# A later slot for root scalings, for the closings of the short convolutions and for the base of the inverse, in a hybrid encoder trunk

## The chip, the core and the metric

The kernel runs on one core of one Trainium2 chip. TensorE (PE) does the matmuls, VectorE (DVE), ScalarE (ACT) and GpSimd (POOL) do the rest, SyncE (SP) starts the DMAs. The metric is device time in microseconds (us), the median of several runs. Each engine works through its own queue in program order. An instruction waits in its queue until what it needs is there, and everything behind it on that engine waits with it.

## The reference

One layer for two groups of frames (256 new positions and 64 positions of a running stream, 320 columns together), with a sandwich of RMS norms around two sub-layers. Cut to what matters here:

```python
def gdn_mixer(qkv, z, ...):                       # 8 heads of 128
    qkv = silu(causal_dwconv(qkv, buf, w_sc))     # width 4
    q = l2norm(heads(q)) * HEAD_DIM ** -0.5
    k = l2norm(heads(k))
    o, s = gated_delta_chunked(q, k, v, g, beta, s0)
    o = o * rsqrt(mean(o * o) + EPS) * onorm_g
    return o * silu(z)

def gated_delta_chunked(q, k, v, g, beta, s0):
    m = strict_lower(kb @ k.T * decay)
    tmat = solve(I + m, I)                        # unit lower triangular
    u, w = tmat @ (v * beta), tmat @ (kb * exp(G))
    for each chunk:
        v_new = u - w @ s
        o = (q * exp(G)) @ s + qk @ v_new
        s = s * g_last + k_dec.T @ v_new

def conformer_conv(...):                          # 8 groups of 128 channels
    u = causal_dwconv(h_val * sigmoid(h_gate), width 31)
    return silu(group_layernorm(u))

def trunk_layer(x, ...):
    p = rmsnorm(x) @ w_in
    x = x + rmsnorm(concat(conformer_conv(p), gdn_mixer(p)) @ w_out)
    gu = causal_dwconv(rmsnorm(x) @ w_up, width 3)
    return x + rmsnorm((silu(gate) * up) @ w_down)
```

## The kernel before

Activations lie with channels on the partitions and the 320 columns along the free axis. Each float32 product is made of three: `load_split` loads a weight tile `w` by DMA, ACT rounds it to `whi` (L214) and DVE takes the rest `wlo` (L215). Per 128x128 piece PE then runs whi times the rounded activation (L230), whi times the activation's rest (L231) and wlo times the rounded activation (L234). Each of these is one **dense matmul** of 128x320. `block_matmul` runs 48 of them for each 128 output columns of w_in, and the rest of the layer (w_out, w_up, w_down) works alike.

While w_in runs, in the order of `PLAN`, small steps of the two mixers are threaded between the dense matmuls. They are written as Python generators, called jobs:

- `conv_tail` (one per channel group): transposes into the PSUM tile `pt_c` (L575), statistics on DVE (L577 and after), an inverse square root on POOL (`grs` L583, `gnm` L584), then three scalings on ACT (`un`, L588), and transposes back.
- `gdn_tail` (one per head h0 to h7): transposes of k, q and v (L674 to L678), squares on ACT (L680, L682), `tq6` (L684, L685), the inverse square root and its products on POOL (`sc`, L687 to L693), then the scalings `kd`, `kds` and `vh` on ACT (L697 to L702), then the products `pk`, `pks` (L706, L710) on PE and `np`, `at` on DVE.
- `pair` (one per two heads, pairs 0 to 3): `base_inverse` inverts 16x16 blocks on DVE (L745 to L759, after a trip of `np` through DRAM into `dn`), then after a delay `levels` merges blocks to 32, 64 and 128 on PE and ACT (`pz`, `zh` L784, `px` L789, `zq` L808, `px` L813, ...), then `post` runs the recurrence: `ks` (L872) on PE, `rhs` (L876) on DVE, `pvns` (L884) on PE, `ks1` (L893), `rh1` (L896) on DVE, and so on. It ends with an inverse square root on POOL (`t1`, L921 to L925), the scalings `ot` (L929) on ACT, and, later, the transposes `pt_o` (L938).

The steps share PSUM: the tiles `pt_c`, `pt_c2`, `tkq` and `pt_o` take turns in two banks (pool `ps_t`), and most others in four (pool `ps_g`).

**What sets the order.** `tick` counts the dense matmuls; the text gives places in the program as that count ("dense 1800"). Every `GAP` = 20 dense matmuls it holds a slot: the jobs that are due are advanced by one step each, in a limited number, and each step is issued behind the dense matmul of the slot. A step ends in `yield wait, g, t`: the job is due again `wait` dense matmuls later, at the next slot after that. A fourth value marks the step that follows. A step marked "scale" is one that needs an inverse square root from POOL: it isn't taken in the first loop over the due jobs but in the second one, and is issued behind the newest ACT instruction of the slot. Since the second loop looks at the mark as it stands after the first loop, a job whose step in the first loop has just yielded "scale" is advanced again there, in the same slot: POOL's root and the ACT scaling that needs it are then issued in one slot.

`qkv_block` (three per head) makes a projection and the short convolution: `qb`, `cq` on ACT (L627) and three multiply-adds on DVE (L629), then two SiLU on ACT (L631 to `kq` or `vT`, L632 to `kqs` or `vts`), all issued at once, with raised priority. `conv_block` does a channel group's gate, and its 32 taps (L557 to L560) are handed to DVE a few per slot.

Of the kernel before, what the change touches and what calls it, by code (L numbers as in the profile page):

```python
# [30 lines left out]
GAP = 20  # L31
# [69 lines left out]
def trunk_kernel(ctx, tc, ins, outs):  # L101
# [11 lines left out]
    jobs = []  # L113
# [4 lines left out]
    def next_tap(front=None):  # L118
        left, fn = taps.pop(0)
        with ExitStack() as e:  # L120
            if front is not None:
                e.enter_context(tc.issue_after(front))
            fn()
        left[0] -= 1

    def advance(job, behind=None):
        with tc.issue_after(behind or dense[0]), tc.high_priority(offset=PRI_J):
            try:
                wait, job[2], job[3], *kind = next(job[1])
                job[0] = dense[1] + wait  # L130
                job[4] = kind
            except StopIteration:
                jobs.remove(job)
        return next(i for i in reversed(nc.cur_bb.bb.instructions) if i.engine == dense[0].engine)

    def start(gen, wait, g=0, t=0):
        job = [dense[1] + wait, gen, g, t, []]
        jobs.append(job)
        return job
# [5 lines left out]
    def newest(engine, n0):  # L145
        return next((i for i in reversed(nc.cur_bb.bb.instructions[n0:]) if i.engine == engine), None)

    def tick(mm):
        dense[0] = mm.ins
        dense[1] += 1  # L150
        if dense[1] % GAP == 0:
            g, t0, behind, due = 0, held_t[0], dense[0], []
            t = t0
            n0 = len(nc.cur_bb.bb.instructions)
            for job in sorted(jobs, key=lambda j: j[0]):
                if job[0] <= dense[1] and g + job[2] <= 4 and t + job[3] <= 2:
                    g += job[2]
                    t += job[3]
                    due.append(job)
            for job in due:  # L160
                if not job[4]:
                    behind = advance(job, behind)
            scalar = newest(mybir.EngineType.Activation, n0)
            for job in due:
                if "scale" in job[4]:
                    with ExitStack() as e:
                        if scalar is not None:
                            e.enter_context(tc.issue_after(scalar))
                        advance(job)
            held_t[0] = t - t0  # L170
            front = newest(mybir.EngineType.DVE, n0)
            for _ in range(min(pace[0], len(taps))):
                next_tap(front)
# [15 lines left out]
    def pv(name, a=None, b=None):  # L189
        o, w = PAR[name]  # L190
        if a is None:
            return par[:, o:o + w]
        return par[:, o + a:o + (a + 1 if b is None else b)]
# [103 lines left out]
    def in_block(b, name):  # L297
        if b in ready:
            return ready.pop(b)
        ps = ps_p.tile([P, 512], F32, tag="p", name=name)  # L300
        block_matmul(ps[:, 0:T], ins["w_in"][b], hx, (8, 8))
        return ps
# [10 lines left out]
    with tc.tile_pool(name="xp", bufs=1) as xp:  # L313
# [25 lines left out]
        with tc.high_priority(offset=PRI_E):  # L339
# [25 lines left out]
            for k in range(KB):  # L365
                x = xt[k // 4][:, k % 4, :]
# [32 lines left out]
        def first_norm():  # L399
            rr, _ = rstd([ssum[:, 0, :], ssum[:, 1, :]])  # L400
            yield 36, 1, 0
            S.copy(rb, rstd_rows(rr)[0])

        job = start(first_norm(), 24, 1)
# [10 lines left out]
    gate = {}  # L415
# [185 lines left out]
    NS = 2  # L601
# [16 lines left out]
    def qkv_block(b, dst, dsts, i):  # L618
        psq = in_block(16 + b, "psq")
        qb = qbufs[i % 2]  # L620
        with tc.high_priority(offset=PRI_E):
            S.copy(qb[:, 4, 0:3], pv("s_qkv", b * 3, b * 3 + 3))
            V.tensor_tensor(qb[:, :, 3:67], psq[:, 0:T].rearrange("p (s i) -> p s i", s=5),
                            rb.rearrange("p (s i) -> p s i", s=5), ALU.mult)
            S.copy(qb[:, 1:4, 0:3], qb[:, 0:3, 64:67])
            cq = cb.tile([P, 5, 64], F32, tag="cq", name="cq")
            S.activation(cq, qb[:, :, 0:64], AF.Identity, scale=pv("w_sc", b * 4))  # L627
            for t in range(1, 4):
                V.scalar_tensor_tensor(cq, qb[:, :, t:t + 64], pv("w_sc", b * 4 + t), cq, ALU.mult, ALU.add)  # L629
            S.copy(nqkv[:, b], qb[:, 3:5, 64:67])  # L630
            S.activation(dst, cq[:, 0:4].rearrange("p s i -> p (s i)"), AF.Silu)  # L631
            S.activation(dsts, cq[:, 4], AF.Silu)  # L632

    def gdn_pre(h, st):
        s = h % NS
        while s and h // NS > 1 and "free" not in sts[h // NS - 2]:
            advance(pairs[h // NS - 2])
        if s == 0:
            st["kqs"] = gd.tile([P, 2, P], F32, tag="kqs", bufs=3, name="kqs")
            st["vts"] = gd.tile([P, P], F32, tag="vts", bufs=1, name="vts")  # L640
        kq = gd.tile([P, 2, TP], F32, tag="kq", bufs=5, name="kq")
        vT = gd.tile([P, TP], F32, tag="vT", bufs=1, name="vT")
        cols = slice(s * TS, (s + 1) * TS)
        qkv_block(8 + h, kq[:, 0, :], st["kqs"][:, 0, cols], h)
        qkv_block(h, kq[:, 1, :], st["kqs"][:, 1, cols], h + 1)
        qkv_block(16 + h, vT, st["vts"][:, cols], h)
        return kq, vT


    def gdn_tail(h, st, kq, vT):  # L650
        s = h % NS
        while not gate or (s and "kq" not in st) or (h // NS > 1 and "free" not in sts[h // NS - 2]):
            yield GAP, 1 + 2 * s, 1
        if s == 0:
            st["kd"] = gd.tile([P, S_, P], F32, tag="kd", name="kd")
# [6 lines left out]
        kd, vh, at, kqs = st["kd"], st["vh"], st["at"], st["kqs"]  # L662
# [64 lines left out]
    def base_inverse(bt, st):  # L727
        i = bt % 2
        nb = 8 * NI
        nc.sync.dma_start(nscr[i][:, 0:16384].rearrange("a (p f) -> p a f", f=128), st["np"])  # L730
        dn_t = gd.tile([nb, 272], F32, tag="dn", bufs=1, name="dn")
        wi_t = gd.tile([nb, 272], F32, tag="wi", bufs=1, name="wi")
        tmp_t = gd.tile([nb, 512], F32, tag="tmp", bufs=1, name="tmp")
        dn, wi = (t[:, 0:256].rearrange("p (r c) -> p r c", c=16) for t in (dn_t, wi_t))
        nc.sync.dma_start(dn, blocks(nscr[i], 128))
        G.memset(wi_t, 0.0)
        G.memset(wi_t[:, 0:256:17], 1.0)
        yield 2 * GAP, 0, 0

        d8, w8 = (t.rearrange("p (b x) -> p b x", b=2)[:, :, 0:128].rearrange("p b (r c) -> p b r c", c=16)[:, :, :, 0:8]  # L740
                  for t in (dn_t, wi_t))
        for r in range(6, -1, -1):
            m = 7 - r
            tmp = tmp_t[:, 0:2 * m * m].rearrange("p (b s c) -> p b s c", b=2, s=m)
            V.tensor_tensor(tmp, w8[:, :, r + 1:8, r + 1:8],  # L745
                            d8[:, :, r, r + 1:8].unsqueeze(3).to_broadcast((nb, 2, m, m)), ALU.mult)
            V.tensor_reduce(w8[:, :, r, r + 1:8], tmp.rearrange("p b s c -> p b c s"), AX.X, ALU.add)
            if r in (3, 0):
                yield GAP, 0, 0
        tmp = tmp_t.rearrange("p (r c s) -> p r c s", r=8, c=8)  # L750
        x = dn_t[:, 0:64].rearrange("p (r c) -> p r c", c=8)
        V.tensor_tensor(tmp, dn[:, 0:8, 8:16].unsqueeze(2).to_broadcast((nb, 8, 8, 8)),
                        wi[:, 8:16, 8:16].rearrange("p s c -> p c s").unsqueeze(1).to_broadcast((nb, 8, 8, 8)), ALU.mult)
        V.tensor_reduce(x, tmp, AX.X, ALU.add)
        yield GAP, 0, 0
        V.tensor_tensor(tmp, wi[:, 0:8, 0:8].unsqueeze(2).to_broadcast((nb, 8, 8, 8)),
                        x.rearrange("p s c -> p c s").unsqueeze(1).to_broadcast((nb, 8, 8, 8)), ALU.mult)
        V.tensor_reduce(wi[:, 0:8, 8:16], tmp, AX.X, ALU.add)
        V.tensor_copy(dn, wi.rearrange("p a b -> p b a"))  # L759
        nc.sync.dma_start(blocks(wscr[i], 128)[0:nb], wi)  # L760
        nc.sync.dma_start(blocks(wscr[i], 128)[nb:2 * nb], dn)
        wtp = gd.tile([P, 2, NI, P], F32, tag="wtp", name="wtp")
        nc.sync.dma_start(wtp.rearrange("p a b f -> p (a b) f"), wscr[i][:, 0:16384].rearrange("a (p f) -> p a f", f=128))
        st["w"] = wtp
# [199 lines left out]
    tails, convs, pairs, sts = {}, {}, {}, []  # L964
    for step in plan:
        kind, i = step[0], int(step[1:] or 0)
# [6 lines left out]
        elif kind == "h":  # L973
            if i % NS == 0:
                if i:
                    ready[24 + i] = in_block(24 + i, "psq")
                st = {}
# [147 lines left out]
    job = start(second_norm(), 68, 1)  # L1125
# [189 lines left out]
```

## Time and profile before

| what | value |
|---|---|
| median of 3 runs | 1498.56 us (1497.97 to 1499.13) |
| the profiled execution's own span, first to last instruction | 1497.8 us |
| PE's mean granted clock over it | 0.997 |
| DVE, ACT, POOL busy over the span | 996.1, 727.9, 229.2 us |
| the stretch 38 to 549 us (w_in, the mixers, w_out) | PE busy 501.80 of 511.00 us |
| DMA, mean over the span | 150 GB/s |

The profile counts an engine as busy while an instruction runs; for PE the matmuls are pipelined, so that a dense matmul has a duration of 309 ns in the profile while the next one starts some 147 ns after it. "Idle before" is the time for which an engine stood still ahead of an instruction, with the instruction that ended this. The clock that the profile grants PE is given as a share of full speed, as a mean over a window. Of the time around the profiled span only the difference to the runs' median is known: 1498.56 - 1497.8 = 0.8 us.

### The profile page before, as it was taken

The numbers are of one execution on the slowest core, as the hardware profiler recorded it, in microseconds if no ns is written. First come the engines' busy times: TensorE is split into PE (matmuls) and PEld (weight loads), VectorE is DVE, ScalarE is ACT, GpSimd is POOL, SyncE is SP. The second block draws the span as 40 slices with busy tenths as digits, with TensorE's granted clock in tenths as the row PEclk, the third lists the DMA queues.
The fourth block names the chain that finished last, engine by engine and source line by source line (L and its number), as shares of the span: only waits on it lengthen the run. The fifth ranks groups of instructions, "written<-read, shape, count | busy, mean of one in ns | idle before, by whom it ended". The sixth has DMA issues, their size and how long they took to land.

```text
span 1497.8 us, 27263 instructions
## 1 busy us (share of the span) xinstructions
PE 1481.6 (99%) x10609; PEld 1460.4 (98%) x10610; DVE 996.1 (67%) x1816; ACT 727.9 (49%) x1329; POOL 229.2 (15%) x390
## 2 busy tenths in 40 slices
PE   9999999999999999999999999999999999999998
PEld 8999999989999999999999999999999999999997
DVE  6779886978989678766345666445666545666554
ACT  7764556554544565544434444334444333444453
POOL 0111101120010000332002222002223101222101
PEclk9999999999999999999999999999999999999999
DMA  8435453544434744444554444455444455444453
GB/s 289 142 128 157 141 155 120 146 139 134 130 106 142 221 151 141 148 149 128 149 169 151 151 154 134 140 156 164 154 152 141 136 146 173 153 146 152 130 152 118
DMA packets 98281, 224.22 MB, mean 150 GB/s; under 512 B 18792, under 2 KB 39528, under 8 KB 98152
## 3 DMA queue, kind: packets, MB, share of 16 engines
q1 hardware_dynamic: 98008, 222.45, 47.7%
q8 instruction: 83, 1.36, 0.4%
q14 instruction: 46, 0.38, 0.1%
q10 hardware_dynamic: 144, 0.03, 0.0%
HBM read 215.33 MB, written 7.12 MB: 149 GB/s over the span
## 4 chain that ended last, share of the span: by engine, by line
PE 86%; DVE 6%; ACT 3%; DMA 2%; issue 2%; POOL 1%; SPq 0%; ACTq 0%; DVEq 0%
PE psu L234 13%; PE psu L231 13%; PE psu L230 13%; PE psdn L230 7%; PE psdn L231 6%; PE psdn L234 6%; PE psq L234 2%; PE psq L230 2%; PE psq L231 2%; PE psm L231 2%; PE psm L230 2%; PE psm L234 2%; DVE wlo L215 1%; PE psu L1108 1%; PE ps_first L395 1%
## 5 line engine op out<-in xcount | busy, mean ns | idle before, releaser
L214 ACT CAST whi<-w 128x1024 fp32r<-128x1024 f32 (+2 forms) x440 | 412.6, 940 | 481.7 <-PE psu L231 169.0
L215 DVE TENSOR_TENSOR wlo<-w,whi 128x1024 fp32r<-128x1024 f32 (+2 forms) x440 | 477.0, 1085 | 199.0 <-ACT whi L214 127.8
L230 PE MATMUL psu<-hi,whi 128*128 128x320 f32 x1344 | 397.0, 309 | 0.0
L231 PE MATMUL psu<-lo,whi 128*128 128x320 f32 x1344 | 397.0, 309 | 0.0
L230 PEld LDWEIGHTS psu<-hi,whi 128*128 128x128 f32 x1344 | 252.3, 188 | 0.0
L231 PEld LDWEIGHTS psu<-lo,whi 128*128 128x128 f32 x1344 | 252.3, 188 | 0.0
L234 PE MATMUL psu<-hi,wlo 128*128 128x320 f32 x1344 | 224.4, 309 | 0.0
L234 PEld LDWEIGHTS psu<-hi,wlo 128*128 128x128 f32 x1344 | 204.0, 188 | 0.0
L231 PE MATMUL psdn<-gl,whi 128*128 128x320 f32 x660 | 195.9, 310 | 0.0
L1141 POOL COPY nffn<-fbuf 128x2 f32<-128x2 f32 x88 | 101.5, 1153 | 586.9 <-DVE fbuf L1139 583.7
L1139 DVE TENSOR_TENSOR fbuf<-psu,rb 128x256 f32<-128x256 f32 x88 | 37.3, 424 | 168.9 <-PE psu L234 168.9
L230 PE MATMUL psdn<-gh,whi 128*128 128x320 f32 x480 | 142.8, 309 | 0.0
L231 PEld LDWEIGHTS psdn<-gl,whi 128*128 128x128 f32 x660 | 123.9, 188 | 0.3
L230 PE MATMUL psq<-hh,whi 128*128 128x320 f32 x352 | 106.2, 315 | 0.0
L231 PE MATMUL psq<-hl,whi 128*128 128x320 f32 x352 | 104.1, 309 | 0.0
L230 PEld LDWEIGHTS psdn<-gh,whi 128*128 128x128 f32 x480 | 90.1, 188 | 0.0
L234 PE MATMUL psdn<-gh,wlo 128*128 128x320 f32 x480 | 89.9, 309 | 0.0
L234 PEld LDWEIGHTS psdn<-gh,wlo 128*128 128x128 f32 x480 | 75.3, 188 | 0.0
L230 PEld LDWEIGHTS psq<-hh,whi 128*128 128x128 f32 x352 | 66.1, 188 | 0.3
L231 PEld LDWEIGHTS psq<-hl,whi 128*128 128x128 f32 x352 | 66.1, 188 | 0.2
L560 DVE SCALAR_TENSOR_TENSOR cvt<-ub,par,cvt 128x320 f32<-128x320 f32 x120 | 65.2, 543 | 0.2
L1184 DVE TENSOR_TENSOR y<-y,psdn 128x320 f32<-128x320 f32 x45 | 22.0, 488 | 59.1 <-PE psdn L234 59.1
(356 smaller groups left out, 2483.3 us busy)
## 6 DMA issues: line engine op xcount, KB each, us to landing
w<-in_w_up SPq DMA_DIRECT2D x176, 512.0 KB, 3.6
w<-in_w_in SPq DMA_DIRECT2D x88, 512.0 KB, 3.9
w<-in_w_down SPq DMA_DIRECT2D x64, 384.0 KB, 3.1
w<-in_w_down SPq DMA_DIRECT2D x64, 320.0 KB, 3.0
w<-in_w_out SPq DMA_DIRECT2D x32, 320.0 KB, 3.8
w<-in_w_out SPq DMA_DIRECT2D x16, 384.0 KB, 3.2
w<-in_w_first SPq DMA_DIRECT2D x6, 512.0 KB, 6.9
wtp<-wsp SPq DMA_DIRECT2D x4, 640.0 KB, 6.0
```

What stands on the lines that cost most here:

```text
L214: S.copy(hi[:, 0:width], w[:, 0:width])
L215: V.tensor_tensor(lo[:, 0:width], w[:, 0:width], hi[:, 0:width].bitcast(F32), ALU.subtract)
L230: tick(PE.matmul(ps, wh, xh, start=(first and k0 + j == 0), stop=False))
L231: tick(PE.matmul(ps, wh, xl, start=False, stop=False))
L234: tick(PE.matmul(ps, lo[:, j * P:(j + 1) * P], xh, start=False, stop=(final and k0 + j == nk - 1)))
L395: tick(PE.matmul(ps, w, xh, start=(k == 0 and wt is hi), stop=(k == KB - 1 and wt is lo)))
L560: return lambda: V.scalar_tensor_tensor(acc, x, w, acc, ALU.mult, ALU.add)
L1108: PE.matmul(pss[i][:, 0:T], wt[:, o:o + P], x, start=(k == 0 and n == 0), stop=(k == KB - 1 and n == 2))
L1139: V.tensor_tensor(buf[:, 2:258], psu[:, 0:TP], rb2[:, 0:TP], ALU.mult)
L1141: G.tensor_copy(nffn[:, b, 0, :], buf[:, 256:258])
L1184: V.tensor_tensor(y[:, n, :], y[:, n, :], psd[:, 0:T], ALU.add)
```

## The change

Three edits, in `tick`, in `qkv_block` with `gdn_tail`, and in `base_inverse`.

```diff
@@ tick @@
+            done = []
...
             for job in due:
                 if not job[4]:
                     behind = advance(job, behind)
-            scalar = newest(mybir.EngineType.Activation, n0)
+                    done.append(job)
+            last_of = [i for x in (mybir.EngineType.Activation, mybir.EngineType.DVE)
+                       if (i := newest(x, n0)) is not None]
             for job in due:
-                if "scale" in job[4]:
+                if job[4] and job not in done:
                     with ExitStack() as e:
-                        if scalar is not None:
-                            e.enter_context(tc.issue_after(scalar))
+                        for i in last_of:
+                            e.enter_context(tc.issue_after(i))
                         advance(job)
@@ qkv_block @@
+        def silu():
             S.activation(dst, cq[:, 0:4].rearrange("p s i -> p (s i)"), AF.Silu)
             S.activation(dsts, cq[:, 4], AF.Silu)
+            yield from ()
+
+        job = start(silu(), GAP // 2)
+        job[4] = ["scale"]
+        return job
@@ gdn_pre, gdn_tail @@
-        qkv_block(8 + h, kq[:, 0, :], st["kqs"][:, 0, cols], h)
...
+        return kq, vT, [qkv_block(8 + h, kq[:, 0, :], st["kqs"][:, 0, cols], h),
...
-    def gdn_tail(h, st, kq, vT):
+    def gdn_tail(h, st, kq, vT, silus):
...
-        while not gate or (s and "kq" not in st) or ...
+        while not gate or any(j is silu for j in jobs for silu in silus) or (s and "kq" not in st) or ...
@@ base_inverse (at its first yield, after r = 3 and r = 0, and after L754) @@
-        yield 2 * GAP, 0, 0
+        yield 2 * GAP, 0, 0, "long"
...
-                yield GAP, 0, 0
+                yield GAP, 0, 0, "long"
```

First, a marked step is taken in the second loop only if its job wasn't advanced in the first, so that a root's scaling now waits for a later slot; and it is issued behind the newest ACT and the newest DVE instruction of that slot. Second, the two SiLU that close a short convolution become a job of their own, marked in the same way, due half a gap later; `gdn_tail` doesn't begin before its head's three are done. Third, the steps of `base_inverse` are marked too ("long"), so that they are issued behind the other ACT and DVE steps of their slot. No arithmetic changes. Line numbers grow by 3 to 9: L214 becomes L217, L215 L218, L697 L706, L702 L711, L784 L793, L808 L817, L876 L885.

As the programs are built, the number of instructions on each engine stays as it was but for the loads of ACT's function tables, 9 before and 11 now. The steps on PE stand later in the program: pair 0's and pair 3's chains by 40 dense matmuls, pair 2's by 20 (its first `px` at dense 1800 before, 1820 now), pair 1's by 20 at its begin and 40 at its end. POOL's order is the same.

On ACT, around the first merge of pair 2 (`zh`, then `zq`), this stood before; `vT`, `vts` are SiLU of head 5, the rows from L680 to L702 are head 5's `gdn_tail`:

```order
400 L631 ACTIVATE vT<-cq 128x256
401 L632 ACTIVATE vts<-cq 128x64
402 L784 ACTIVATE zh<-pz,cst 128x80
403 L214 CAST whi<-w 128x1024
...
412 L685 ACTIVATE tq_4133<-ssq_598,eps 128x3
413 L214 CAST whi<-w 128x1024
414 L697 ACTIVATE kd<-tkq,sc 128x128
415 L702 ACTIVATE vh<-tv,sc 128x128
...
420 L808 COPY zq<-pz 32x5x32 x2
421 L214 CAST whi<-w 128x1024
```

And now:

```order
405 L636 ACTIVATE vT<-cq 128x256
406 L637 ACTIVATE vts<-cq 128x64
407 L217 CAST whi<-w 128x1024
408 L793 ACTIVATE zh<-pz,cst 128x80
...
418 L694 ACTIVATE tq_4162<-ssq_598,eps 128x3
419 L217 CAST whi<-w 128x1024
420 L817 COPY zq<-pz 32x5x32 x2
421 L706 ACTIVATE kd<-tkq,sc 128x128
422 L711 ACTIVATE vh<-tv,sc 128x128
...
428 L217 CAST whi<-w 128x1024
```

`zh` has moved one slot down, behind a weight cast, and `zq` has moved ahead of head 5's scalings.

On DVE, around the right-hand side `rhs` of pair 2's recurrence, this stood before; the rows with `tmp`, `dn` and `wi` are the base inverse of pair 3:

```order
514 L752 TENSOR_TENSOR tmp<-dn,wi 40x512
515 L560 SCALAR_TENSOR_TENSOR odd<-ub_587,par,odd 128x320
516 L754 TENSOR_REDUCE dn<-tmp 40x64
517 L876 SCALAR_TENSOR_TENSOR rhs<-ks,neG,vh 64x128
518 L756 TENSOR_TENSOR tmp<-wi,dn 40x512
519 L533 TENSOR_TENSOR sg<-psgate,rb 128x320
520 L876 SCALAR_TENSOR_TENSOR rhs<-ks,neG,vh 64x128
521 L758 TENSOR_REDUCE wi<-tmp 40x8x8
522 L215 TENSOR_TENSOR wlo<-w,whi 128x1024
```

And now:

```order
511 L218 TENSOR_TENSOR wlo<-w,whi 128x1024
...
514 L885 SCALAR_TENSOR_TENSOR rhs<-ks,neG,vh 64x128
515 L563 SCALAR_TENSOR_TENSOR odd<-ub_587,par,odd 128x320
516 L885 SCALAR_TENSOR_TENSOR rhs<-ks,neG,vh 64x128
517 L754 TENSOR_TENSOR tmp<-wi,dn 40x50
...
521 L754 TENSOR_TENSOR tmp<-wi,dn 40x98
522 L218 TENSOR_TENSOR wlo<-w,whi 128x1024
...
525 L761 TENSOR_TENSOR tmp<-dn,wi 40x512
...
527 L763 TENSOR_REDUCE dn<-tmp 40x64
```

Both halves of `rhs` now stand ahead of the last three rows of the recursion and of the four long rows that close the base inverse (L761 to L767, before L752 to L758).

On ACT, around the tails of heads 0 and 1, this stood before; the cast in row 135 makes the first weights of `psz` of block z2, which PE needs at dense 657:

```order
134 L685 ACTIVATE tq_1258<-ssq_597,eps 128x2
135 L214 CAST whi<-w 128x1024
136 L697 ACTIVATE kd<-tkq,sc 128x128
...
140 L680 ACTIVATE vh,ssq_597<-tkq 128x128 x2
...
148 L685 ACTIVATE tq_1316<-ssq_597,eps 128x3
149 L622 COPY qb_594<-par 128x3
```

And now, to the cast that makes the same weights:

```order
133 L694 ACTIVATE tq_1256<-ssq_597,eps 128x2
134 L636 ACTIVATE kq<-cq 128x256
135 L637 ACTIVATE kqs<-cq 128x64
136 L706 ACTIVATE kd<-tkq,sc 128x128
137 L689 ACTIVATE vh,ssq_597<-tkq 128x128 x2
...
142 L694 ACTIVATE tq_1312<-ssq_597,eps 128x3
...
149 L706 ACTIVATE kd<-tkq,sc 128x128
...
158 L637 ACTIVATE kqs<-cq 128x64
159 L217 CAST whi<-w 128x1024 x3
```

The cast that stood ahead of both heads' scalings now stands behind all of them and behind the SiLU of the next short convolution.

More of the change, by code (lines that the diff above doesn't have):

```diff
@@ L643, in gdn_pre @@
         cols = slice(s * TS, (s + 1) * TS)
-        qkv_block(8 + h, kq[:, 0, :], st["kqs"][:, 0, cols], h)
-        qkv_block(h, kq[:, 1, :], st["kqs"][:, 1, cols], h + 1)
-        qkv_block(16 + h, vT, st["vts"][:, cols], h)
-        return kq, vT
-    def gdn_tail(h, st, kq, vT):
+        return kq, vT, [qkv_block(8 + h, kq[:, 0, :], st["kqs"][:, 0, cols], h),
+                        qkv_block(h, kq[:, 1, :], st["kqs"][:, 1, cols], h + 1),
+                        qkv_block(16 + h, vT, st["vts"][:, cols], h)]
+    def gdn_tail(h, st, kq, vT, silus):
         s = h % NS
-        while not gate or (s and "kq" not in st) or (h // NS > 1 and "free" not in sts[h // NS - 2]):
+        while not gate or any(j is silu for j in jobs for silu in silus) or (s and "kq" not in st) or (h // NS > 1 and "free" not in sts[h // NS - 2]):
             yield GAP, 1 + 2 * s, 1
@@ L754, in base_inverse @@
         V.tensor_reduce(x, tmp, AX.X, ALU.add)
-        yield GAP, 0, 0
+        yield GAP, 0, 0, "long"
         V.tensor_tensor(tmp, wi[:, 0:8, 0:8].unsqueeze(2).to_broadcast((nb, 8, 8, 8)),
```

## The prediction

> **What bounds the kernel now.** I read the page's busy times first, then two windows of the span, then PE's waits in the first of them, then PE's granted clock around the two longest waits. PE has almost no idle time:
>
> ```profile
> PE 1481.6 (99%) x10609; PEld 1460.4 (98%) x10610; DVE 996.1 (67%) x1816; ACT 727.9 (49%) x1329; POOL 229.2 (15%) x390
> ```
>
> So a change to ACT's and DVE's order can bring no more than PE's waits, and what comes with them. The windows give the time, then PE's, PEld's, DVE's, ACT's and POOL's busy time, PE's clock and the DMA:
>
> ```profile
> 38.00:549.00 511.00, 501.80 (x3992) 489.13 (x3991) 415.37 (x865) 288.41 (x723) 54.86 (x115) 0.99 0.47 144
> 549.00:1480.00 931.00, 930.50 (x6331) 927.90 (x6330) 548.03 (x906) 407.68 (x552) 165.38 (x261) 1.00 0.47 147
> ```
>
> From 549 us on, PE stands still for 0.5 us in 931, at full clock: nothing is to be had there, and the change doesn't touch that code. All is decided between 38 and 549 us, where PE is idle for 511.0 - 501.8 = 9.2 us. Its waits there (engine, what waits, what it waited for: us in total, times, longest):
>
> ```profile
> PE px L789 <- ACT zh L784: 2.9, 2, 2.0
> PE pvns L884 <- DVE rhs L876: 1.9, 1, 1.9
> PE psm L1052 <- ACT m L1000: 1.1, 1, 1.1
> PE pt_o L938 <- ACT un L588: 0.7, 1, 0.7
> PE px L813 <- ACT zq L808: 0.6, 1, 0.6
> PE psm L1054 <- DVE wlo L215: 0.6, 1, 0.6
> PE pst L256 <- ACT sq L1023: 0.5, 1, 0.5
> PE psm L1052 <- ACT bh L238: 0.3, 1, 0.3
> PE psg L476 <- DVE gt L459: 0.3, 1, 0.3
> ```
>
> Five waits, in rows 1, 2, 4 and 5, are in the mixers' steps: 2.9 + 1.9 + 0.7 + 0.6 = 6.1 us. The other five (psm, pst, psg: 1.1 + 0.6 + 0.5 + 0.3 + 0.3 = 2.8 us) belong to w_out, its norm and the gates. There the order of ACT and DVE stays nearly as it was, so I leave these 2.8 us in.
>
> The idle time isn't the whole price. Behind the two longest waits, which ended at 315.46 and 352.18 us (start, duration, engine, line, operation, idle before), the clock falls:
>
> ```profile
> 315.46 0.48 PE L789 MATMUL px<-wtp,zh 32*16 32x16 f32 x38 [1.95 <-ACT zh L784]
> ```
> ```profile
> 352.18 0.46 PE L884 MATMUL pvns<-rhs,wtp 128*128 128x128 f32 x2 [1.86 <-DVE rhs L876]
> ```
>
> The windows, PE's clock third from the right:
>
> ```profile
> 315.50:317.50 2.00, 2.00 (x73) 1.96 (x74) 0.80 (x4) 1.71 (x5) 0.00 (x0) 0.51 0.45 107
> 317.50:319.50 2.00, 2.00 (x11) 2.00 (x10) 1.40 (x8) 0.00 (x0) 0.00 (x0) 0.64 0.53 199
> 352.00:354.00 2.00, 1.82 (x10) 1.85 (x11) 1.97 (x4) 1.93 (x9) 0.00 (x0) 0.77 0.16 21
> 354.00:356.00 2.00, 2.00 (x10) 2.00 (x9) 2.00 (x5) 1.23 (x3) 0.00 (x0) 0.50 0.47 88
> 356.00:358.00 2.00, 2.00 (x16) 2.00 (x16) 1.49 (x3) 0.00 (x0) 0.00 (x0) 0.88 0.68 203
> ```
>
> PE counts as busy in these rows, but only 10 matmuls start in 354 to 356 us where 2.0 us hold some 13.6 at the usual 147 ns. The clock that is lost is, behind the first wait, 2 x 0.49 + 2 x 0.36 = 1.70 us, and behind the second 2 x (0.23 + 0.50 + 0.12) = 1.70 us. A lost share of the clock is lost time, so these two waits cost 3.40 us on top. If the clock is halved throughout, each stretch is 3.4 us long: by these rows from 315.54 to 318.94 and from 353.08 to 356.48. [...]
>
> [...]
>
> **The change part by part.** I go through the five waits, with what stood in front of PE in each.
>
> First, the shorter wait for zh, of pair 0. ACT ran all of a head's squares and then, in the same slot, zh:
>
> ```profile
> 157.68 0.35 ACT L784 ACTIVATE zh<-pz,cst 128x80 f32<-128x80 f32 x1
> ```
>
> Directly ahead of it ran the six squares and the two `tq` of head 3. Now both the squares and all the scalings of that head stand a slot earlier, and two weight casts with slack of their own are between. Removed: 2.9 - 2.0 = 0.9 us. If two such steps meet again in one slot, the same 0.9 us is back.
>
> Second, zh of pair 2, for the px at 315.46 us:
>
> ```profile
> 314.63 0.42 ACT L631 ACTIVATE vT<-cq 128x256 f32<-128x256 f32 x1 [1.03 <-DVE cq L629]
> 314.96 0.24 ACT L632 ACTIVATE vts<-cq 128x64 f32<-128x64 f32 x1
> 315.10 0.31 ACT L784 ACTIVATE zh<-pz,cst 128x80 f32<-128x80 f32 x1
> ```
>
> zh was queued behind two SiLU that wait for DVE's short convolution. The SiLU keep their place, but zh comes a slot later (20 x 0.147 = 2.9 us) with one cast of 1.05 us more ahead of it. So 2.0 us of wait becomes about 2.9 - 1.05 - 2.0 = -0.2, that is, hardly any wait: removed 2.0 us, and its 1.7 us of clock.
>
> Third, zq of pair 2, in two rows:
>
> ```profile
> 327.93 0.37 ACT L697 ACTIVATE kd<-tkq,sc 128x128 f32<-128x128 f32 x1 [1.81 <-POOL sc L690]
> ```
> ```profile
> 330.09 0.59 ACT L808 COPY zq<-pz 32x160 f32<-32x160 f32 x2
> ```
>
> ACT stood for 1.81 us for POOL's root and then made seven scalings, 327.93 to 330.09, ahead of zq. Now zq stands ahead of them: 2.16 + 1.81 us earlier, against 0.6 us of wait. Removed 0.6 us.
>
> Fourth, rhs of pair 2, for the pvns at 352.18 us:
>
> ```profile
> 350.18 1.06 DVE L756 TENSOR_TENSOR tmp<-wi,dn 40x512 f32<-40x512 f32 x1
> 351.17 0.48 DVE L533 TENSOR_TENSOR sg<-psgate,rb 128x320 f32<-128x320 f32 x1
> 351.68 0.36 DVE L876 SCALAR_TENSOR_TENSOR rhs<-ks,neG,vh 64x128 f32<-64x128 f32 x1
> ```
>
> The second half of rhs waited behind a base-inverse step of 1.06 us, and three more stood ahead (L752, L754 and the last of the recursion). After the change all four long steps stand behind rhs. They don't vanish: they stand ahead of rh1, which PE needs 40 dense matmuls after pvns's slot (third rival). Removed 1.9 us, and 1.7 us of clock.
>
> Fifth, pt_o, whose PSUM bank was held by un while POOL made its root; un is now a slot away from its root, and pt_o stands 60 dense matmuls later. Removed 0.7 us. Sum of the five: 6.1 us of waits and 3.4 us of clock, **9.5 us** gained at the most.
>
> Now the costs. After the change there are three places without cover.
>
> (a) The cast for z2 at dense 657. Before:
>
> ```profile
> 101.43 1.04 ACT L214 CAST whi<-w 128x1024 fp32r<-128x1024 f32 x1
> ```
> ```profile
> 108.90 0.37 ACT L702 ACTIVATE vh<-tv,sc 128x128 f32<-128x128 f32 x1 [1.82 <-POOL sc L689]
> ```
> ```profile
> 111.39 1.04 ACT L214 CAST whi<-w 128x1024 fp32r<-128x1024 f32 x1
> 112.14 0.31 PE L230 MATMUL psz<-hh,whi 128*128 128x320 f32 x1
> ```
>
> The cast at 101.43 us was done 9.7 us before PE used it at 112.14. Now it stands behind everything that ACT did up to 111.39. That run loses the cast itself (1.04 us) and between none and most of the 1.82 us wait, since more work lies between root and scaling: it ends between 111.39 - 1.04 = 110.35 and 108.5 us, the cast 1.04 later, at 109.6 to 111.4. PE gets there earlier too, since the pk and pks of both heads (ten matmuls of 128x256, some 0.2 us each) go behind dense 657: at about 110.3. So the new wait is between 0 and 1.1 us; I take 0.4.
>
> (b) Steps of the chains that now meet other work: rh1 of pair 2 behind the long steps, and pair 0's steps at dense 1140 to 1180, which now share slots with weight casts and short convolutions. The nearest rows are the waits of before, 0.6 to 2.0 us each. Between nothing and two of the long kind with their clock, 2 x (1.9 + 1.7) = 7.2 us; I take two of the smallest, 1.2 us.
>
> (c) Two more table loads on ACT, since SiLU now falls between exponentials of the gates. One is
>
> ```profile
> 98.23 1.28 ACT L631 ACT_TABLE_LOAD   x1
> ```
>
> so 2.6 us of ACT, at some 60 to 78 us, where ACT is far from full. The only tight step there is gt's chain, which has PE waiting 0.3 us already: 0 to 1.3 us more, I take 0.3. [...]
>
> Sum: 9.5 - 0.4 - 1.2 - 0.3 = **7.6 us** gained. The profiled span goes from 1497.8 to 1490.2; the runs' median lay 0.8 us above it, so 1498.6 - 7.6 = **1491.0 us**.
>
> **The rivals.** First, *the change doesn't do what it says where it counts.* Issuing behind the newest ACT and DVE instruction only orders a step within its slot; a scaling may still be queued ahead of a root's completion, as un is before w_out, and chains moved by 20 or 40 dense matmuls meet new neighbours as often as the old ones. For it: the chain steps that now stall in five places are a matter of coincidence, and every chain is shuffled. Against it: zq and rhs stand clearly ahead of what held them. Time: new waits of the same 9.5 us, 1498.6.
>
> Second, *the waits go but the half clock stays*, because the dips have another cause or fall elsewhere: 6.1 - 1.9 = 4.2 us gained, 1494.4. Against it: both dips start where the waits end. [...]
>
> Third, on the other side, *DVE becomes the bound of the pairs' recurrence.* DVE has little room there:
>
> ```profile
> 345.00:360.00 15.00, 13.14 (x85) 12.88 (x84) 14.33 (x30) 6.43 (x18) 0.00 (x0) 0.89 0.40 119
> ```
>
> **For it:** DVE is busy for 14.33 of 15.00 us (third busy time), and the four long steps that now stand behind rhs are two multiplications like the one of 1.06 us above and two sums of at most that, up to 4.2 us, of which two stand ahead of rh1. PE reaches the matmul on rh1 two slots, 40 x 0.147 = 5.9 us, behind pvns's; the stretch of half clock that gave DVE time before is gone. The base inverses of pairs 1, 2 and 3 fall on the recurrences of pairs 0, 1 and 2: three places. A wait of 2.5 us in each, with 1.7 us of clock, is 3 x 4.2 = 12.6 us, and -9.5 + 12.6 gives 1498.6 + 3.1 = 1501.7. It decides for slower from 1.5 us a place on: 3 x (1.5 + 1.7) = 9.6. **Against it:** DVE's work is the same in sum, and some of its time there was lost in waiting for casts that ACT held back behind the scalings (this is of 300 to 372 us):
>
> ```profile
> DVE wlo L215 <- ACT whi L214: 7.7, 3, 3.3
> ```
>
> With the casts ahead of the scalings, a part of these 7.7 us comes back to DVE.
>
> **How the numbers follow.** The forecast has 0.60, the first rival 0.13, the second 0.12, the third 0.10; 0.05 is left for more than the sum, if some of the 2.8 us in w_out goes as well. The range goes from 1487.0 (9.5 us gained, no new wait, and 2 of the 2.8 us) to 1499.5, which takes in the first two rivals and the ends of (a) and of (b) (-9.5 + 1.1 + 7.2 + 1.3 is still +0.1); the third is left out. A measurement of this kernel tells about 0.2% from no change, which is 3.0 us, so faster means under 1495.6 and slower over 1501.5. Faster: the forecast, most of the second rival, and the 0.05, together 0.76. Same: the first rival and the rest of the second, 0.14. Slower: the third, 0.10.
>
> **What would show it.** In the profile of the changed kernel, PE's waits between 38 and 549 us should no longer name zh, zq, rhs and un, or with under 1 us each, the idle time should fall from 9.2 to some 5 us, and the mean clock over 38 to 372 us should have no dip behind a mixer step. The first casts of psz of z2 should end within 1 us of PE's arrival. ACT should wait less for POOL's sc and gnm, and DVE less for whi. What would make it wrong: a single new wait of about 1.9 us with a window of half clock costs 3.6 us, half of the gain; a new wait on rh1 or on wlo between 340 and 365 us is the third rival; waits on the same tiles at later places, the first.

## The result and the profile after

The changed kernel takes 1489.16 us (median of 4 runs, 1488.93 to 1489.85), against 1498.26 us before on the same chip: a ratio of 0.9941, 95% interval 0.9928 to 0.9953. That is 9.1 us less; 7.6 were forecast, 1491.0 us, with a range from 1487.0 to 1499.5. The profiled execution has a span of 1487.6 us, 10.2 less than before.

In every run with both figures the time is 1.7 to 1.9 us longer than the span of the same execution (here 1489.37 against 1487.6). So the execution profiled before, with its span of 1497.8, took some 1499.6 us, about 1.3 over the median of that kernel. The 0.8 us given ahead of the prediction mixes two executions, and the two profiles show about 1 us more than the medians do.

PE's waits between 38 and 549 us are now these (engine, what waits, what it waited for: us in total, times, longest):

```profile
PE psm L1063 <- DVE wlo L218: 1.1, 2, 0.8
PE psz L233 <- ACT whi L217: 0.6, 1, 0.6
PE pst L259 <- ACT sq L1032: 0.5, 1, 0.5
PE psg L479 <- DVE gt L462: 0.2, 1, 0.2
```

None of zh, zq, rhs and un is left. What remains is w_out, its norm and the gates as before, 1.8 us in place of 2.8, and one new wait, for the cast of block z2. Two windows of the same profile (us, PE, PEld, DVE, ACT and POOL busy, PE's clock, DMA):

```profile
38.00:549.00 511.00, 508.49 (x4061) 496.31 (x4060) 425.37 (x884) 294.57 (x731) 56.43 (x115) 1.00 0.47 146
...
306.00:372.00 66.00, 66.00 (x602) 64.31 (x602) 59.12 (x136) 36.33 (x96) 9.77 (x15) 1.00 0.48 145
```

PE's idle time fell from 9.2 to 511.00 - 508.49 = 2.5 us, so by 6.7 us, and the clock stays full (1.00 from 306 to 372 us, second row) where it was halved twice, 3.4 us more. Together that is 10.1 of the 10.2 us between the two spans: nothing else is needed to explain them.

ACT's waits for POOL, in the same 511 us, fell from 46.4 to 27.4 us (un 20.0 to 8.7, the scalings of `gdn_tail` 16.3 to 10.3, ot 10.1 to 8.4). So the later slot takes away a part of them only; kd alone waits as long as before (6.9 and 7.0).

The single places, in the timeline (start, duration, engine, line, operation; idle before). First `zh` and `zq` of pair 2 on ACT:

```profile
313.91 0.42 ACT L636 ACTIVATE vT<-cq 128x256 f32<-128x256 f32 x1 [1.03 <-DVE cq L632]
314.24 0.24 ACT L637 ACTIVATE vts<-cq 128x64 f32<-128x64 f32 x1
314.38 1.04 ACT L217 CAST whi<-w 128x1024 fp32r<-128x1024 f32 x1
315.32 0.31 ACT L793 ACTIVATE zh<-pz,cst 128x80 f32<-128x80 f32 x1
...
324.79 0.29 ACT L817 COPY zq<-pz 32x160 f32<-32x160 f32 x1
325.23 0.37 ACT L706 ACTIVATE kd<-tkq,sc 128x128 f32<-128x128 f32 x1 [0.15 <-POOL sc L699]
```

ACT still waits 1.03 us for DVE's short convolution ahead of vT, but zh is done at 315.63, and PE begins px at 316.15: 0.5 us to spare, where before it waited 2.0. zq stands ahead of the scalings, and the scalings wait 0.15 us for POOL in place of 1.81.

Then `rhs` and `rh1` of pair 2 on DVE, with PE's product on rh1:

```profile
345.52 0.36 DVE L885 SCALAR_TENSOR_TENSOR rhs<-ks,neG,vh 64x128 f32<-64x128 f32 x1
...
349.00 1.05 DVE L761 TENSOR_TENSOR tmp<-dn,wi 40x512 f32<-40x512 f32 x1
...
354.46 0.60 DVE L905 SCALAR_TENSOR_TENSOR rh<-ks,neG,vh 128x128 f32<-128x128 f32 x2
```

```profile
355.87 0.60 PE L864 MATMUL pvn<-rh,wtp 128*128 128x128 f32 x4
```

rhs is done at 345.9, 2.3 us before pvns at 348.22. rh1, behind the long steps, is done at 355.06, 0.8 us ahead of PE. The third rival was that near. Last, the new wait:

```profile
109.59 1.03 ACT L217 CAST whi<-w 128x1024 fp32r<-128x1024 f32 x1
```

```profile
110.68 0.41 PE L233 MATMUL psz<-hh,whi 128*128 128x320 f32 x1 [0.58 <-ACT whi L217]
```

PE came at 110.10 us and the cast was done at 110.62.

### The profile page after: what moved, and what is told of

The parts are those of the page before. It is cut to its first block, busy times and chain, and to the rows that moved or that the text cites. A ratio compares the mean times of both kernels' runs of the same rounds, so it can differ in the third digit from the quotient of the medians.

```text
span 1487.6 us, 27264 instructions
## 1 busy us (share of the span) xinstructions
PE 1478.6 (99%) x10610; PEld 1458.2 (98%) x10610; DVE 996.6 (67%) x1816; ACT 730.8 (49%) x1331; POOL 230.5 (15%) x390
## 4 chain that ended last, share of the span: by engine, by line
PE 95%; ACT 2%; DVE 1%; issue 1%; DMA 0%; POOL 0%; DVEq 0%; ACTq 0%; POOLq 0%
PE psu L237 13%; PE psu L234 13%; PE psu L233 13%; PE psdn L233 7%; PE psdn L234 7%; PE psdn L237 7%; PE psq L233 3%; PE psq L234 3%; PE psq L237 3%; PE psm L237 2%; PE psm L233 2%; PE psm L234 2%; PE psu L1117 1%; PE psv L233 1%; PE psgate L233 1%; PE ps_first L398 1%
## 5 line engine op out<-in xcount | busy, mean ns | idle before, releaser
L217 ACT CAST whi<-w 128x1024 fp32r<-128x1024 f32 (+2 forms) x440 | 412.6, 940 | 488.5 <-PE psu L234 169.7
L218 DVE TENSOR_TENSOR wlo<-w,whi 128x1024 fp32r<-128x1024 f32 (+2 forms) x440 | 477.2, 1085 | 191.4 <-ACT whi L217 123.9
```

The costliest lines, as they stand in the source:

```text
L217: S.copy(hi[:, 0:width], w[:, 0:width])
L218: V.tensor_tensor(lo[:, 0:width], w[:, 0:width], hi[:, 0:width].bitcast(F32), ALU.subtract)
```

## The experiments

**Which edit brings the gain.** Four kernels, three rounds each, on one chip, where the kernel before took 1497.93 us. First only the edit of `tick`:

```diff
 # against the changed kernel
-        def silu():
             S.activation(dst, cq[:, 0:4].rearrange("p s i -> p (s i)"), AF.Silu)
             S.activation(dsts, cq[:, 4], AF.Silu)
-            yield from ()
-
-        job = start(silu(), GAP // 2)
-        job[4] = ["scale"]
-        return job
...
-        yield 2 * GAP, 0, 0, "long"
+        yield 2 * GAP, 0, 0
```

> Only the first edit (a marked step is taken in a later slot than the one that marked it, behind the newest ACT and DVE instruction); the SiLU of the short convolutions are issued at once as before, base_inverse isn't marked. Theory A, the true later slot of the root scalings carries nearly the whole gain, since it alone moves all chains by 20 to 40 dense matmuls and puts rhs of pair 2 ahead of the long base-inverse steps: 1489 to 1491 us, no PE wait over 0.7 us on zh, zq, rhs or un, no window of reduced clock between 38 and 549 us. Theory B, each edit heals its own site: rhs of pair 2 (or zh behind the SiLU) still waits 1.9 us with a half clock behind it, 1493 to 1495 us.

Measured: 1488.16 us (1487.95 to 1488.53), ratio 0.9931, interval 0.9917 to 0.9946. PE's waits:

```profile
PE psm L1056 <- DVE wlo L218: 1.0, 1, 1.0
PE pst L259 <- ACT sq L1025: 0.5, 1, 0.5
PE psg L479 <- DVE gt L462: 0.3, 1, 0.3
```

Theory A holds and B falls: the first edit alone removes all five waits, and the time is even 0.8 us under A's window. The new wait for z2's cast isn't there either. In this kernel's program rhs stands ahead of the four long steps though base_inverse isn't marked, since the chain of pair 2 itself has moved. And built without the condition on the newest DVE instruction, the first edit alone gives the same program order on every engine, so that "a later slot" is the part that works.

Without the third edit:

```diff
-        yield 2 * GAP, 0, 0, "long"
+        yield 2 * GAP, 0, 0
...
-                yield GAP, 0, 0, "long"
+                yield GAP, 0, 0
```

> The change without its third edit (base_inverse unmarked). Theory A: within 1 us of the full change, 1488.5 to 1490.5 us. Theory B: the wait for rhs of pair 2 and its half clock are back, 1.9 + 1.7 us: 1492 to 1494 us.

Measured: 1490.62 us (1489.76 to 1490.93), ratio 0.9947, interval 0.9932 to 0.9961; a little outside A's window and under B's. PE didn't wait for rhs. PE's idle time in the profile is 3.6 us, and the waits that the full change's profile didn't show are in w_out and its norm (m 0.8, an accumulation of the norm 0.6, bh 0.3). Without the second edit (the SiLU issued at once as above, the marks of base_inverse left in):

> The change without its second edit (the SiLU issued at once, 9 table loads). Theory A: within 1 us of the full change, 1488.5 to 1490.5 us. Theory B: zh of pair 2 waits behind vT again, 2.0 + 1.7 us: 1492 to 1494 us.

Measured: 1488.49 us (1487.30 to 1490.24), ratio 0.9934, interval 0.9919 to 0.9949. No wait for zh, none for z2's cast. So the SiLU job isn't needed for the gain. The late cast needs it, but not it alone: it is there with the first and the second edit together (this change and the run before), not with the first alone, and not in the next run, which has the second without the first. Last, root scalings in their root's slot again, with the other two edits:

```diff
-                if job[4] and job not in done:
+                if "scale" in job[4] or (job[4] and job not in done):
```

> The change with root scalings taken again in the slot that issues their root (second and third edit stay). Theory A: most of the gain is gone, PE waits on zh and zq of 0.6 us or more are there and at least one window of half clock: 1494 to 1498 us. Theory B: only the sites of the scalings (zh of pair 0, zq, un: 0.9 + 0.6 + 0.7 us) come back: 1491 to 1492 us.

Measured: 1495.14 us (1493.81 to 1497.01), ratio 0.9981, interval 0.9971 to 0.9990. Its profile's largest waits of PE:

```profile
PE psm L1061 <- ACT m L1009: 1.6, 1, 1.6
PE pks L719 <- ACT vh L711: 1.2, 2, 1.0
PE pt_o L947 <- ACT un L591: 0.7, 1, 0.7
PE px L822 <- ACT zq L817: 0.6, 1, 0.6
```

The time lies in A's window. zq and un are back at their old 0.6 and 0.7 us, zh has 0.5, a little less than A wanted, and a new place (pks, whose bank vh holds) has 1.2. The mean granted clock of this execution is 0.998, against 1.0 in the full change's first profile, so some of the clock is lost again; where, no row here shows. The longest wait, the one of 1.6 us for m, is in w_out and not at a mixer step. The wait for rhs and the long one for zh are not back: these two the other edits hold off by themselves, without the first.

**Which scalings.** The first edit again, alone, split in two, three rounds each against 1498.55 us:

```diff
 # only gdn_tail waits for a later slot
-        yield LAG_WAIT, 1 + s, 1, "scale"
+        yield LAG_WAIT, 1 + s, 1, "later"
...
-                if job[4] and job not in done:
+                if "scale" in job[4] or (job[4] and job not in done):
```

> Of the first edit only the part for gdn_tail: kd, kds and vh wait for a later slot than their root; un of the channel groups and ot at a pair's end are taken in their root's slot as before. Theory H, this part carries the gain, since it delays pk, np and so every pair's chain by a slot or two, which takes zh, zq and rhs off their neighbours: 1488 to 1491 us, no wait over 0.5 us on zh, zq or rhs, no half clock before 480 us; the wait of pt_o for un (0.7 us) may stay. Rival, the parts share it: 1492 to 1495 us.

Measured: 1490.27 us (1490.04 to 1491.70), ratio 0.9952, interval 0.9937 to 0.9967. That is in H's window. PE's clock between 38 and 549 us is 1.00 as a mean; there is one wait of 0.5 us for rhs of pair 0, none for un. The counterpart marks gdn_tail's step "same" and tests for that:

> The counterpart: un and ot wait for a later slot, the scalings of gdn_tail are taken in their root's slot as before. Theory H: 1495 to 1498.5 us, with waits on zh, zq or rhs of 0.6 us or more. Rival, the parts share it: 1492 to 1495 us.

Measured: 1495.68 us (1495.40 to 1498.58), ratio 0.9984, interval 0.9974 to 0.9994. In its profile, which is of the slowest of the ten runs:

```profile
PE pvns L886 <- DVE rhs L878: 2.5, 2, 2.2
PE px L791 <- ACT zh L786: 2.4, 2, 1.5
```

Theory H holds by both times. The scalings of gdn_tail alone bring 8.3 us on this chip, where the whole first edit brought 9.8 and 9.4 on two others. un and ot alone bring 2.9, by the interval between 0.9 and 3.9.

How the scalings of gdn_tail do it is argued from the program: a slot's delay there delays pk, np, the base inverse and the whole chain of each pair, and zh, zq and rhs meet other neighbours. For un either part is enough: PE doesn't wait for it in q_tails, where un is in its root's slot and ACT waits 16.3 us for the root (20.0 before), nor in q_rest, where un comes a slot later and ACT still waits 19.2. So PE's wait can go with ACT's nearly as long as it was. No run delays the chains by a slot and leaves the scalings beside their root. So it isn't shown whether any such delay would have done as well.

**What a wait costs beyond itself.** Two kernels, one execution each, with zh made several times over:

```diff
-        S.activation(zh, pz, AF.Identity, scale=cv("odd", P, 1))
+        for _ in range(12):
+            S.activation(zh, pz, AF.Identity, scale=cv("odd", P, 1))
```

> The full change, with the ACT step that makes zh written 12 times instead of once (the same values), in all four pairs: PE's wait for zh becomes some 0.5 to 3 us, by the slack of 0.5 to 2.5 us that each pair has. [...]

PE waited for zh four times, 8.3 us in all (2.60, 0.28, 2.26 and 3.17). The three long ones ended at 167.95, 325.25 and 400.78 us. The stretches of 3.41 us in which they ended, each followed by the next:

```profile
166.28:169.69 3.41, 1.74 (x75) 1.71 (x76) 3.38 (x13) 2.35 (x9) 0.76 (x2) 1.00 0.61 206
169.69:173.11 3.42, 3.42 (x15) 3.42 (x15) 2.48 (x6) 2.56 (x5) 0.00 (x0) 0.50 0.38 89
323.30:326.71 3.41, 1.46 (x73) 1.43 (x74) 2.03 (x5) 2.46 (x8) 0.00 (x0) 1.00 0.52 159
326.71:330.12 3.41, 3.41 (x16) 3.37 (x16) 3.38 (x8) 3.08 (x18) 0.00 (x0) 0.50 0.50 151
398.39:401.80 3.41, 1.02 (x70) 0.99 (x71) 1.78 (x3) 2.48 (x7) 0.00 (x0) 1.00 0.51 163
401.80:405.21 3.41, 3.41 (x15) 3.41 (x15) 2.95 (x8) 1.71 (x5) 0.00 (x0) 0.50 0.42 120
```

Behind each, the next 3.41 us are at half clock (0.50), which loses 1.7 us. The execution's mean granted clock, 0.997, leaves room for three such stretches (5.1 of 1500.5 us) and not for a fourth behind the wait of 0.28 us. The sum: 1489.2 + 8.3 + 3 x 1.7 = 1502.6 us; measured 1502.27. So here waits of 2.26 to 3.17 us cost themselves and 1.7 us more each; in the 3.41 us ahead of the first half clock PE was idle for 1.67 us (3.41 - 1.74, first row). With zh made 18 times:

> As before with zh made 18 times: waits of some 1.5 to 5 us. Theory C: 3.41 us of half clock behind nearly all of the four waits, 1.7 us each on top of their sum. [...]

Waits of 2.78, 0.42, 2.48 and 3.33 us; 1505.61 us. The first, which ended at 170.71 us, had no half clock behind it:

```profile
166.05:169.46 3.41, 1.88 (x13) 1.61 (x11) 3.41 (x12) 3.15 (x10) 0.79 (x2) 1.00 0.60 202
169.46:172.87 3.41, 2.16 (x77) 2.13 (x78) 2.51 (x7) 2.76 (x10) 0.00 (x0) 1.00 0.40 92
172.87:176.29 3.42, 3.42 (x41) 3.18 (x40) 3.42 (x9) 2.28 (x6) 0.00 (x0) 1.00 0.49 158
```

Why it had none isn't shown. The wait of 2.48 us was followed by 3.41 us at 0.50 (329.89, in the last section), and the one of 3.33, which ended at 405.10, by twice as much:

```profile
404.98:408.39 3.41, 3.29 (x77) 2.86 (x77) 3.20 (x7) 1.28 (x6) 0.00 (x0) 0.50 0.35 90
408.39:411.81 3.42, 3.42 (x29) 3.02 (x30) 0.96 (x7) 0.57 (x2) 0.00 (x0) 0.50 0.03 11
411.81:415.00 3.19, 3.19 (x46) 2.96 (x46) 2.02 (x7) 2.51 (x6) 1.35 (x2) 1.00 0.02 5
```

"Nearly all" was wrong, then. The sum, 1489.2 + 9.0 + 3 x 1.7 = 1503.3, is 2.3 us under the one time measured; these 2.3 us are not attributed.

**The cast for z2.** One execution, with only block z2's weights loaded and rounded at a priority above the jobs':

```diff
+        boost[0] = 2200 if h == 2 else PRI_W
         psz = in_block(40 + h, "psz")
+        boost[0] = PRI_W
```

> The full change, with the weights of block z2 loaded and rounded at a raised priority, so that the cast that PE needs at dense 657 stands ahead of the scalings of heads 0 and 1 again (PE's order is the same). Theory E, the new wait of 0.58 us there is the price of the cast's place behind the scalings: it vanishes, the other waits stay, span 0.4 to 0.7 us shorter. Rival: the cast's delay is in its DMA or in the buffer that PE frees, and the wait stays; or the scalings are late for pk, and a wait appears there.

Measured: 1488.46 us, span 1486.7, 0.9 us under the full change's. The cast runs at 101.04 us, and PE starts psz without a wait:

```profile
109.75 0.31 PE L233 MATMUL psz<-hh,whi 128*128 128x320 f32 x1
```

Theory E holds for the wait (0.6 us); the span is shorter by more than the 0.4 to 0.7 expected, and a single time can't settle a gain of that size.

**How near DVE is.** One execution, with the first long step of the base inverse (L761) made four times:

```diff
-        V.tensor_tensor(tmp, dn[:, 0:8, 8:16]...
+        for _ in range(4):
+            V.tensor_tensor(tmp, dn[:, 0:8, 8:16]...
```

> The full change with the first of the four long steps of base_inverse made four times (the same values), so that some 2.9 us more of DVE stand ahead of rh1 of pair 2. In the profile of the full change rh1 was ready 0.8 us before PE's product on it. Theory G, DVE is that near to being the bound of the recurrence: PE waits for rh1, or for a wlo just ahead of it, some 2.1 us between 345 and 365 us, and a half clock may follow (1.7 us more). Rival: DVE's backlog has other room (its taps can wait), and no wait of PE over 0.5 us appears there.

Measured: 1497.72 us, more than 7 us over the median of the full change on that chip (1490.40), and 5.9 by the spans of the two profiles (1495.9 and 1490.0), but not where G had it. PE's three largest waits:

```profile
PE pt_c L578 <- DVE cvt L557: 3.2, 4, 1.3
PE px L799 <- ACT zh L794: 1.2, 1, 1.2
PE psgate L237 <- DVE wlo L218: 0.9, 1, 0.9
```

and at pair 2, where 2.1 us were expected, rh1 was just in time:

```profile
362.91 0.59 DVE L906 SCALAR_TENSOR_TENSOR rh<-ks,neG,vh 128x128 f32<-128x128 f32 x2
```

```profile
363.36 0.69 PE L865 MATMUL pvn<-rh,wtp 128*128 128x128 f32 x4
```

Twelve more steps of 1.05 us, 12.6 us of DVE, cost 6 to 7 us, spread over late taps (pt_c waits for cvt), zh, weights and a short convolution (tv waits for vT, 0.9 us): PE, delayed earlier, came later to rh1. G was wrong about the place. The rival was right about it, since between 345 and 365 us PE doesn't wait at all; but the taps, which it took for DVE's spare room, couldn't all wait. That DVE has little room is shown, that rh1 is the place isn't.

**The full change against its first edit.** Five rounds each on one chip, before 1498.42 us:

> The full change once more, on one chip with p1_again. Theory A (the first edit carries the gain): 1488 to 1490 us. Theory F, the second edit adds a cost of its own, since it alone puts the cast for z2 behind the SiLU and brings the two table loads: 0.5 to 1 us longer than p1_again. Rival: the 1 us between earlier runs was the chip, and both are the same within 0.3 us.

> Only the first edit, once more, on one chip with after_again. Theory A and F: 1487.5 to 1489 us, 0.5 to 1 us under after_again. Rival: the same within 0.3 us.

Measured: 1490.40 us (1489.01 to 1492.04) for the full change, ratio 0.9949, interval 0.9937 to 0.9961, and 1489.06 us (1487.42 to 1492.80) for the first edit, ratio 0.9937, interval 0.9925 to 0.9950. Both are just over their windows, and the intervals overlap widely: inconclusive. One reason is w_out, where the profile of the full change has other waits than the first time:

```profile
PE psm L1061 <- ACT whi L217: 1.7, 1, 1.7
PE psm L1063 <- DVE wlo L218: 1.1, 1, 1.1
PE psm L1061 <- ACT m L1009: 0.6, 1, 0.6
```

With bh's 0.3 these are 3.7 us, against 1.1 in the first profile of the same program: 2.6 us, where the spans differ by 2.4 (1490.0 and 1487.6). The first edit's second profile has the same waits for whi and wlo, 1.7 and 1.1 us, and there PE's clock is at half in w_out:

```profile
516.00:518.00 2.00, 2.00 (x9) 2.00 (x8) 1.71 (x5) 1.82 (x5) 0.00 (x0) 0.50 0.90 300
```

So the half clock isn't gone for good: single executions can still have it in w_out.

## Why the prediction was right, step by step

- **The five waits, 6.1 us.** Right: all are gone. Where it spoke of rhs, it showed the long steps moved behind it, as they are, and left open which edit does that; the runs show that the third edit isn't needed, because the first has moved the chain. For un it gave two reasons, the root a slot away and pt_o later; PE has no wait for un in q_tails, with the root where it was, nor in q_rest, with un and ot alone moved, so either is enough.
- **The half clock, 3.4 us.** Right in the profiled execution: both dips are gone with their waits, and with zh made 12 times three waits of 2.26 to 3.17 us were each followed by 3.41 us at 0.50. Why some waits are followed by it and others aren't is not shown. Mis-sized against the median, though: the execution that I summed from was a long one, some 1499.6 us. In 24 runs of the kernel before on two chips the mean granted clock was 0.997 in four (mean 1500.3 us), 0.998 or 0.999 in twelve (1498.4) and 1.0 in eight (1497.2). The first and the last are 3.1 us apart, near the 3.4 of two stretches of half clock. On the chip of the split (13 runs) the time doesn't go with the clock: none is at 0.997, eleven at 0.998 or 0.999 have a mean of 1498.5 us, two at 1.0 one of 1498.0. So that the two stretches are in some executions and not in others is likely, not shown, and how much of the 3.4 us the median had to give stays open; about 1 us less would fit the spans.
- **(a) the cast for z2, 0.4 us.** 0.58 measured, within 0 to 1.1; its place is shown to be the cause (z2_first).
- **(b) new meetings in the chains, 1.2 us.** Nothing: no wait of PE stands there. This is the largest term that failed, and it made the forecast too small where the clock made it too large.
- **(c) two table loads, 0.3 us.** Nothing on PE: gt's wait went from 0.3 to 0.2 us. The loads are there (11 of 1.28 us each), on an ACT that had the time: it is busy for 15.12 of the 18.00 us from 60 to 78 us.
- **w_out, left at 2.8 us.** 1.8 us in the first profile (psm, pst and psg), 4.4 in the second. It varies from one execution to the next of the same program.
- **From the span to the median, 0.8 us.** The same execution takes 1.7 to 1.9 us more than its span. That the forecast of the time was off by 1.8 us only is in part luck: by the profiles, 10.2 us were gained and 7.6 forecast.
- **The rivals.** The first (same number of new waits) and the second (half clock stays) didn't happen. The third didn't either, but rh1 had only 0.8 us to spare, and DVE's waits for whi between 300 and 372 us fell only from 7.7 to 6.9 us.

In sum, by the profiles: PE's idle time was forecast to fall to some 5 us and fell to 2.5. Of the 2.5 us between, (b) is 1.2, (c) 0.3 and w_out, by luck, 1.0. By the medians the gain is 9.1 us and not 10.2, since the execution profiled before was a long one.

## What to carry to other kernels

Where one engine makes a small result for another engine's queue (POOL's root, for which ACT waited 46.4 us in the kernel before), try the consumer one slot later than the producer: here ACT's waits for POOL fell by 19 of 46 us with the full change, though by only 1 with un and ot alone moved (q_rest, 45.2 us). Don't expect a gain in proportion to that. It came on the engine that bounds the kernel, where the chains had happened to meet other work and no longer did. A run that moves the chains in another way would have to show how much of it is the place alone. Check each cast that now stands behind a longer run. Price a long stall of TensorE with the half clock that may follow it: here 3.41 us at 0.50, so 1.7 us, followed waits of 1.45 us (next section) to 3.17 us, and twice that one of 3.33 us, but nothing of the kind followed one of 2.22 us (next section) and one of 2.78 us. And remember that one profile shows only one execution.

## What the runs showed of the hardware that I had not expected

The half clock isn't decided by the length of the wait alone. A wait of 2.22 us for rhs, in the kernel with only un and ot moved, ended at 351.86 us and had no half clock behind it:

```profile
347.90:351.31 3.41, 1.74 (x14) 1.55 (x12) 3.34 (x9) 0.36 (x1) 0.00 (x0) 1.00 0.24 94
351.31:354.73 3.42, 2.87 (x20) 2.90 (x21) 3.36 (x6) 3.30 (x10) 0.00 (x0) 1.00 0.13 18
```

In the same execution a shorter one, of 1.45 us for zh, ended at 315.58 us and had it:

```profile
313.77:317.18 3.41, 1.96 (x78) 1.67 (x77) 2.73 (x7) 2.40 (x8) 0.00 (x0) 1.00 0.54 165
317.18:320.59 3.41, 3.41 (x15) 3.41 (x15) 3.03 (x12) 0.58 (x2) 1.27 (x1) 0.50 0.46 148
```

Nor does PE's idle time in the 3.41 us before decide it alone. With zh made 12 times, half clock followed 1.67 us of it (166.28 above), and the same 1.67 us up to 351.31 were not followed by it. With zh made 18 times, it followed only 0.89 us, behind the wait of 2.48 us that ended at 327.37:

```profile
326.48:329.89 3.41, 2.52 (x69) 1.78 (x71) 0.00 (x0) 1.57 (x10) 0.00 (x0) 1.00 0.54 159
329.89:333.30 3.41, 3.41 (x19) 3.37 (x19) 1.75 (x6) 3.17 (x13) 1.32 (x1) 0.50 0.00 0
```

What decides it isn't shown.
